# A decoder block on one core: two value blocks of the local attention by seven products, bias rows over all partitions, value read-outs behind the next split

## The chip, the cores and the metric

The kernel runs on one core of a Trainium2 chip. The metric is device microseconds of one execution. Engines are named as in the profile: PE is TensorE, DVE is VectorE, ACT is ScalarE, POOL is GpSimd, SP is the engine that issues most loads.

## The reference

One layer of a decoder block for 256 tokens (T) of width 2048 (D). All input projections are columns of one matrix `w_in` of 2048 x 19472:

```python
h = rms_norm(x, g_pre[l])
proj = h @ w_in[l]
y_a = pool_mixer(a_val, a_gate, w_pool[l], pool_scale[l])
y_b = swa_mixer(sq, sk, sv, s_gate)
y_c = gla_mixer(cq, ck, cv, c_lr, c_gate, w_alpha[l], b_alpha[l], g_gla[l])
y_m = mem_attn(mq, m_gate, mem, g_mem[l], w_mem_kv[l])
gates = sigmoid(g_logits.reshape(B, S, 4, 2048) + b_merge[l])
merged = sum of gates[:, :, b] * (y_b @ w_br_b[l]) over the four branches
x = x + rms_norm(merged @ w_out[l], g_post[l])
```

Two parts matter here. The values `sv` of the local (dilated window) attention are `h` times 1536 columns: three blocks of 512 columns, one for each window group. The logits of the gates, `g_logits`, are `h` times 8192 columns: 16 blocks of 512, four for each of the four branches, and `b_merge` is added to them.

## The kernel before, in words

**Numbers.** All large products are computed from float32 operands split into a high and a low part of a reduced type (`R`). A product is three matmuls: high by high, high by low, low by high (`mm3`, L156 to L160). A weight tile of 128 x 1024 is split by `split_w` (L149): ACT copies it to the high part (L152), DVE subtracts to get the low part (L153). There are five buffers for each part (`NB_HILO`, L30), so DVE can be at most five splits ahead of PE. Weights arrive by SP's queue as tiles `raw` of 1 MB (`load_raw`, L144); they share 13 buffers of 8 KB per partition (`e8`) with the normed input and other long-lived tiles.

**Main work.** It is written out as a row of units. `a_block` (L162) makes 256 tokens x up to 512 columns: for each of four weight tiles two splits, and for each split the two halves of the tokens, which accumulate in two PSUM tiles. For 512 columns it takes 16 x 2 x 3 = 96 matmuls of 512 columns and 8 splits. It returns `finish`, which reads both accumulators out. With the argument `late` it calls an earlier block's `finish` behind its own first split (L171 to L174). `b_unit` (L197) makes 128 columns with the weights standing: 16 matmuls of 512 and 16 of 256 columns, two splits, and a read-out of one or more DVE sums. The order is: the memory tokens; eight units cq and ck; the blocks cv0, cv1 and cv2 (values of the linear attention, L700 to L702, each read out at once by ACT, L550); units cg; mq and mg; av and ag (pooling); the blocks sv0, sv1 and sv2 (L835); and 28 units sq, sk and sg. Then come the merges (`bmem`, `bgla`, `bpool`, `bswa`) and the output.

**Two streams woven in.** While the main work runs, two others are advanced. `pull` (L91) steps a queue of small tasks: the chunks of the linear attention (`gla`), heads, pooling groups. `gates` (L109) advances the gate stream: a piece of main work of so many microseconds by plan earns `GATE_SHARE` (L34, 1.13) times as much credit, and each step of the stream costs credit (0.8 or 6.6). The stream starts after the sixth of the units cq and ck and is emptied ahead of the merges (`gates(1e9)`, L897).

**A gate pair** (`gate_pair`, L463) makes two blocks of 512 columns for both halves of the tokens, 2 x 2 products over 2048 = 2 x 1024 rows, by seven products of half size instead of eight (Strassen's scheme in Winograd's form). It has three parts. First p1 (L471 to L481): 16 steps of three matmuls, eight splits `gu`; after half of them ACT copies p1 aside (`p1c`, L480), and the later ones add on in the same PSUM tile. Then eight steps `gt` (L486 to L501): a 1 MB tile of weights, DVE sums on it (L491 with 1024 elements, L492 and L497 with 512 each), two splits, twelve matmuls into q4 to q7. Then sums of the products on DVE (L503 to L509), and two tiles `gv` (L510 to L518), four splits, added to q5. The results go through ACT's tanh (L459) and ACT's queue to memory in HBM, from where the merges read them back by POOL's queue (L918). A pair takes 168 matmuls of 512 columns, and 28 splits.

**The bias.** Ahead of the products, p1 and q5 are started with a matmul that adds the bias (`bias`, L453): its weights are one column of `sel`, repeated 128 times, its other operand is `brow`; both have 48 rows (16 with the high part of the bias, 16 empty, 16 with the low part). There are 16 such matmuls.

Of the kernel before, what the change touches and what calls it, by code (L numbers as in the profile page):

```python
# [8 lines left out]
F32 = mybir.dt.float32  # L9
R = mybir.dt.float32r  # L10
AF = mybir.ActivationFunctionType
ALU = mybir.AluOpType
# [20 lines left out]
NB_C2 = 7  # L33
GATE_SHARE = 1.13  # L34


@with_exitstack
def kernel(ctx, tc, ins, out):
# [388 lines left out]

    brow = cst.tile([48, 512], R, name="brow")
    sel = cst.tile([48, 24], R, name="sel")

# [3 lines left out]
    def bias_prep():  # L434
        pool.tensor_copy(walpha[:, 0:1], xcol[0:16, 0:1])
        pool.tensor_copy(big_cst[:, 0:1], xcol[:, 0:1])
        pool.dma_start(walpha[:], ins["w_alpha"])
        pool.dma_start(big_cst[:], ins["consts"])
        raw = c2("braw", [48, 512])
# [12 lines left out]

    def bias(o, r):  # L453
        ten.matmul(o, lhsT=sel[:, r : r + 1].to_broadcast([48, P]), rhs=brow[:], start=True, stop=False)

# [6 lines left out]

    def gate_pair(b, jj):  # L463


        j0, j1, n = 2 * jj, 2 * jj + 1, f"{b}{jj}"
        w = ins["w_g"]
        p1 = seven(f"p1{n}")
        bias(p1[:], 4 * b + j0)
        p1c = c2(f"p1c{n}", [P, 512])  # L470
        for u in range(4):  # L471
            raw = load_raw(w[b, j0, u], 2048)
            for hf in range(2):
                hi, lo = split_w(raw[:, hf * 1024 : (hf + 1) * 1024], 1024, f"gu{n}{u}{hf}")
                for i in range(2):
                    k = 4 * u + 2 * hf + i
                    ws = slice(i * 512, (i + 1) * 512)
                    mm3(p1[:], *tok(0, k), hi[:, ws], lo[:, ws], False, k % 8 == 7, k >= 8)
                if u == 1 and hf == 1:
                    act.activation(p1c[:], p1[:], AF.Copy)  # L480
                yield 0.8  # L481
        c11 = c2(f"c11{n}", [P, 512])
        put_gate(b, j0, 0, p1[:], c11[:])
        q4, q5, q6, q7 = [seven(f"q{i}{n}") for i in (4, 5, 6, 7)]
        bias(q5[:], 16 + 2 * b + jj)
        for kk in range(8):  # L486
            raw = new_raw()
            r4 = raw[:].rearrange("p (j u c) -> p j u c", j=2, u=2)
            u, cs = kk // 4, slice((kk % 4) * 512, (kk % 4 + 1) * 512)
            sync.dma_start(r4, w[b, j0 : j0 + 2, u : u + 3 : 2, :, cs].rearrange("j u p c -> p j u c"))  # L490
            vec.tensor_tensor(r4[:, :, 0, :], r4[:, :, 0, :], r4[:, 1, :, :], op=ALU.add)  # L491
# [6 lines left out]
            hi, lo = split_w(raw[:, 0:1024], 1024, f"gt{n}{kk}b")  # L498
            mm3(q5[:], *quart(0, kk), hi[:, 0:512], lo[:, 0:512], False, sp)
            mm3(q4[:], *tok(1, kk + 8), hi[:, 512:1024], lo[:, 512:1024], st, sp)  # L500
# [4 lines left out]
        vec.tensor_tensor(c21[:], q4[:], v3[:], op=ALU.subtract)  # L505
        put_gate(b, j0, 1, c21[:], c21[:])
        vec.tensor_tensor(v3[:], q5[:], v3[:], op=ALU.add)
        put_gate(b, j1, 1, v3[:], v3[:])
        vec.tensor_tensor(q5[:], q5[:], p1c[:], op=ALU.add)  # L509
        for u in range(2, 4):  # L510
            raw = load_raw(w[b, j1, u], 2048)
            for hf in range(2):
# [6 lines left out]
        c12 = c2(f"c12{n}", [P, 512])  # L519
        put_gate(b, j1, 0, q5[:], c12[:])  # L520
# [170 lines left out]
    for n in range(8):  # L691
# [404 lines left out]
```

## Time and profile before

| | |
|---|---|
| median of three runs | 1174.86 us (1171.3 to 1175.29) |
| profiled execution | 1172.68 us, of which the span of its instructions is 1170.6 |
| PE, DVE, ACT busy | 1149.8, 961.2, 647.0 us |
| from HBM | 303.94 MB by DMA, 260 GB/s in the mean |

The profile gives for each instruction its line, engine, and the tiles that it writes and reads (out<-in). A matmul's duration is its latency; how fast PE gets on is read from how far apart two matmuls start. The same holds for DVE, whose instructions overlap a little when they follow each other closely. The name of a split shows what it is for: `cv100h` is the high part of the first split of block cv1, `gt103bl` the low part of the second split of gate step 3 of branch 1, first pair (the digits after `gt` are branch, pair and step).

### The profile page before, as it was taken

The numbers are of one execution on the slowest core, as the hardware profiler recorded it, in microseconds if no ns is written. First come the engines' busy times: TensorE is split into PE (matmuls) and PEld (weight loads), VectorE is DVE, ScalarE is ACT, GpSimd is POOL, SyncE is SP. The second block draws the span as 40 slices with busy tenths as digits, with TensorE's granted clock in tenths as the row PEclk, the third lists the DMA queues.
The fourth block names the chain that finished last, engine by engine and source line by source line (L and its number), as shares of the span: only waits on it lengthen the run. The fifth ranks groups of instructions, "written<-read, shape, count | busy, mean of one in ns | idle before, by whom it ended". The sixth has DMA issues, their size and how long they took to land.

```text
span 1170.6 us, 15411 instructions
## 1 busy us (share of the span) xinstructions
PE 1149.8 (98%) x5854; PEld 968.2 (83%) x5854; DVE 961.2 (82%) x1201; ACT 647.0 (55%) x823; POOL 59.0 (5%) x109
## 2 busy tenths in 40 slices
PE   9999999999999999999999999999999999999997
PEld 7887898878888888878888887888788888888887
DVE  7979798999898799889989988987898676777454
ACT  7656456665655555665566556566555543434441
POOL 0010000000101001000000000000000102110000
PEclk9999999999999999999999999999999999999999
DMA  9755679757868688777788777876778988759321
GB/s 356 316 182 193 217 251 343 277 203 281 304 238 284 217 297 289 259 251 263 276 295 315 251 263 271 294 253 231 272 252 303 372 308 306 252 206 381 118 73 73
DMA packets 79946, 303.94 MB, mean 260 GB/s; under 512 B 6224, under 2 KB 8656, under 8 KB 57344
## 3 DMA queue, kind: packets, MB, share of 16 engines
q1 hardware_dynamic: 65568, 268.45, 63.5%
q0 software_dynamic: 8976, 24.91, 6.1%
q10 hardware_dynamic: 5328, 9.60, 2.2%
q8 instruction: 46, 0.75, 0.3%
q14 instruction: 28, 0.23, 0.1%
HBM read 285.11 MB, written 17.83 MB: 259 GB/s over the span
## 4 chain that ended last, share of the span: by engine, by line
PE 76%; DVE 5%; DMA 3%; ACT 2%; issue 2%; DVEq 0%; POOLq 0%; POOL 0%; ACTq 0%
PE q L158 5%; PE q L159 5%; PE q L160 5%; DMA raw<-in_w_g 2%; PE p L158 2%; PE p L159 1%; PE p L160 1%; PE sv2a L159 1%; PE sv0a L158 1%; PE sv0a L160 1%; PE o0a L160 1%; PE sv2a L158 1%; PE o0a L158 1%; PE sv1a L158 1%; PE sv0a L159 1%
## 5 line engine op out<-in xcount | busy, mean ns | idle before, releaser
L491 DVE TENSOR_TENSOR raw<-raw 128x1024 f32<-128x1024 f32 x64 | 78.1, 1220 | 8.9 <-DMA raw<-in_w_g 8.9
L497 DVE TENSOR_TENSOR raw<-raw 128x512 f32<-128x512 f32 x64 | 44.5, 696 | 1.1
L492 DVE TENSOR_TENSOR raw<-raw 128x512 f32<-128x512 f32 x64 | 44.5, 697 | 0.5
L918 POOL DMA_DIRECT2D g<-gd x32 | 17.4, 554 | 98.6 <-DVE merged L926 66.7
L926 DVE TENSOR_TENSOR merged<-merged,g 128x512 f32<-128x512 f32 x24 | 15.5, 686 | 0.0
L710 POOL DMA_DIRECT2D cgd<-cgate x4 | 2.2, 552 | 201.7 <-DVE cgate L241 201.7
L885 POOL DMA_DIRECT2D ybd<-ybt x4 | 2.7, 678 | 174.1 <-DVE ybt L247 174.1
L853 PE MATMUL sp<-k,q 128*128 128x128 f32 (+1 forms) x48 | 10.2, 335 | 1.0 <-DVE k L226 1.0
L861 ACT ACTIVATE s<-s,st 128x384 f32<-128x384 f32 (+1 forms) x8 | 6.2, 769 | 6.7 <-DVE st L860 6.7
L853 PEld LDWEIGHTS sp<-k,q 128*128 128x128 f32 x48 | 7.4, 190 | 2.9 <-DVE k L226 1.4
L856 DVE SCALAR_TENSOR_TENSOR s<-big_cst,sp 128x128 f32<-128x128 f32 (+1 forms) x24 | 7.1, 349 | 2.0 <-PE sp L853 2.0
L246 ACT ACTIVATE xhl<-xn 128x1024 fp32r<-128x1024 f32 x4 | 4.2, 1060 | 7.0 <-DVE xn L330 7.0
L459 ACT ACTIVATE c<-c 128x512 f32<-128x512 f32 x8 | 5.0, 628 | 5.5 <-DVE c L505 3.9
L939 ACT ACTIVATE mTh<-mtp 128x512 fp32r<-128x512 f32 x8 | 4.3, 595 | 6.3 <-PE mtp L937 6.3
L459 ACT ACTIVATE c<-p 128x512 f32<-128x512 f32 x8 | 4.7, 587 | 5.1 <-PE p L160 5.1
L664 POOL TENSOR_TENSOR ms<-ms,half 128x2 f32<-128x2 f32 x4 | 5.7, 1428 | 35.2 <-DVE ms L663 35.2
L879 PE MATMUL po<-pt,sv 128*128 128x256 f32 x24 | 7.2, 384 | 0.2 <-ACT pt L874 0.2
L812 POOL DMA_DIRECT2D yad<-yat x4 | 2.7, 686 | 88.5 <-DVE yat L247 88.5
L360 DVE SCALAR_TENSOR_TENSOR mhl<-mr,vecs,mhl 128x256 fp32r<-128x256 f32 x16 | 6.8, 479 | 0.4 <-issue 0.3
L652 POOL TENSOR_TENSOR sq<-sq 128x256 f32<-128x256 f32 x4 | 4.4, 1106 | 53.0 <-ACT sq L651 53.0
L359 ACT ACTIVATE mhl<-mr,vecs 128x256 fp32r<-128x256 f32 x16 | 6.9, 495 | 0.2 <-DMA mr<-in_memT 0.2
L1003 POOL TENSOR_TENSOR opart<-opart,half 128x1 f32<-128x1 f32 x2 | 1.1, 562 | 116.0 <-DVE opart L1002 116.0
(4603 smaller groups left out, 4582.7 us busy)
## 6 DMA issues: line engine op xcount, KB each, us to landing
raw<-in_w_g SPq DMA_DIRECT2D x112, 1024.0 KB, 5.8
raw<-in_w_sqk SPq DMA_DIRECT2D x24, 1024.0 KB, 6.6
raw<-in_w_sv SPq DMA_DIRECT2D x12, 1024.0 KB, 6.5
raw<-in_w_out SPq DMA_DIRECT2D x12, 1024.0 KB, 9.6
raw<-in_w_cqk SPq DMA_DIRECT2D x8, 1024.0 KB, 15.0
raw<-in_w_cg SPq DMA_DIRECT2D x8, 1024.0 KB, 6.6
raw<-in_w_av SPq DMA_DIRECT2D x8, 1024.0 KB, 5.0
raw<-in_w_ag SPq DMA_DIRECT2D x8, 1024.0 KB, 6.0
```

Source lines behind the costliest of these rows:

```text
L158: ten.matmul(o, lhsT=sh, rhs=wh, start=start, stop=False, skip_group_check=again)
L159: ten.matmul(o, lhsT=sh, rhs=wl, start=False, stop=False, skip_group_check=again)
L160: ten.matmul(o, lhsT=sl, rhs=wh, start=False, stop=stop, skip_group_check=again)
L459: act.activation(dst, src, AF.Tanh, scale=0.5)
L491: vec.tensor_tensor(r4[:, :, 0, :], r4[:, :, 0, :], r4[:, 1, :, :], op=ALU.add)
L492: vec.tensor_tensor(r4[:, 1, 1, :], r4[:, 1, 1, :], r4[:, 0, 0, :], op=ALU.add)
L497: vec.tensor_tensor(r4[:, 0, 1, :], r4[:, 0, 1, :], r4[:, 1, 1, :], op=ALU.add)
L853: ten.matmul(parts[g], lhsT=q3[:, g, it * P : (it + 1) * P], rhs=k3[:, g, :nj], start=True, stop=True)
L856: vec.scalar_tensor_tensor(s[:, g, :], dist[:, g, :], SLOPES[g * 4 + hh], parts[g], op0=ALU.mult, op1=ALU.add)
L879: ten.matmul(po[:], lhsT=sv[g][:, 0, vs], rhs=pt[g][:, 0:T], start=(g == 0), stop=False)
L918: pool.dma_start(gs[t][:], gate_dram[b, j, t][:])
L926: vec.tensor_tensor(m, m, gs[t][:], op=ALU.add)
```

## The change

1. The body of `gate_pair` becomes `seven_products(n, w, put, bias_rows)`, in which the store of a result (`put`) and the bias are parameters. `value_pair` calls it with the value blocks 0 and 1, without a bias, and stores the four results in HBM as they are. It is the fifth of nine pairs in the gate stream. The blocks sv0 and sv1 are no longer main work; sv2 stays. After sv2, the stream is advanced until the value pair is done (by the program's order it has been done by then), and POOL's queue reads the four results into the `sv` tiles.
2. `GATE_SHARE` is 1.38 instead of 1.13, and while sv2 runs `pull` takes twice as many steps.
3. `brow`, `sel` and the tiles that they are made from have 128 rows instead of 48; the additional ones are zero.
4. The blocks cv0 to cv2 are chained by `late`: a block is read out behind the first split of the next one.

```diff
-GATE_SHARE = 1.13
+GATE_SHARE = 1.38
...
+    rate = [1]
+
     def pull(n):
+        n *= rate[0]
...
-    brow = cst.tile([48, 512], R, name="brow")
-    sel = cst.tile([48, 24], R, name="sel")
+    brow = cst.tile([P, 512], R, name="brow")
+    sel = cst.tile([P, 24], R, name="sel")
...
-        one = c2("bsel", [48, 24])
-        vec.tensor_tensor(one[:, 0:16], ident[0:48, 0:16], ident[0:48, 32:48], op=ALU.add)
+        one = c2("bsel", [P, 24])
+        vec.tensor_tensor(one[:, 0:16], ident[:, 0:16], ident[:, 32:48], op=ALU.add)
...
-        ten.matmul(o, lhsT=sel[:, r : r + 1].to_broadcast([48, P]), rhs=brow[:], start=True, stop=False)
+        ten.matmul(o, lhsT=sel[:, r : r + 1].to_broadcast([P, P]), rhs=brow[:], start=True, stop=False)
...
+        def put(t, j, src, tmp):
+            put_gate(b, j0 + j, t, src, tmp)
+
+        return seven_products(f"{b}{jj}", ins["w_g"][b, j0 : j0 + 2], put, (4 * b + j0, 16 + 2 * b + jj))
+
+    sv_dram = {}
+
+    def value_pair():
+        def put(t, j, src, tmp):
+            if src is not tmp:
+                act.activation(tmp, src, AF.Copy)
+            sv_dram[j, t] = spill(f"svd{j}{t}", [P, 512], F32)
+            act.dma_start(sv_dram[j, t][:], tmp)
+
+        return seven_products("sv", ins["w_sv"][0:2], put, None)
+
+    def seven_products(n, w, put, bias_rows):
         p1 = seven(f"p1{n}")
-        bias(p1[:], 4 * b + j0)
+        if bias_rows:
+            bias(p1[:], bias_rows[0])
...
     def all_gates():
-        for jj in range(2):
-            for b in range(4):
-                yield from gate_pair(b, jj)
+        for n in range(9):
+            yield from value_pair() if n == 4 else gate_pair((n - (n > 4)) % 4, int(n > 4))
...
+    late = None
     for j in range(3):
         c0, n = CV_BLOCKS[j]
-        a_block(f"cv{j}", [ins[f"w_cv{j}"][u] for u in range(4)], h_at, n, cv_evac(j))()
+        late = a_block(f"cv{j}", [ins[f"w_cv{j}"][u] for u in range(4)], h_at, n, cv_evac(j), late=late)
+    late()
...
-    for j in range(3):
-        a_block(f"sv{j}", [ins["w_sv"][j, u] for u in range(4)], h_at, 512, sv_evac(j))()
+    rate[0] = 2
+    a_block("sv2", [ins["w_sv"][2, u] for u in range(4)], h_at, 512, sv_evac(2))()
+    while len(sv_dram) < 4:
+        gates(1.0)
+    for j, t in sv_dram:
+        pool.dma_start(sv[j][:, t, :], sv_dram[j, t][:])
...
+    rate[0] = 1
```

The order of the instructions is set when the program is built. At two places that the prediction speaks of, this is what stands there. First ACT, from the last splits of block cv0 to the first gate split after them, before:

```order
L152 ACTIVATE gt003bh<-raw_1291 128x1024
L152 ACTIVATE cv031h<-raw_1273 128x696
L550 ACTIVATE cv<-cv0a_1119 128x348
L550 ACTIVATE cv<-cv0a_1120 128x348
L152 ACTIVATE cv100h<-raw_1336 128x692
L152 ACTIVATE cv101h<-raw_1336 128x692
L152 ACTIVATE gt004ah<-raw_1370 128x1024
```

and now:

```order
L155 ACTIVATE gt004bh<-raw_1316 128x1024
L155 ACTIVATE cv031h<-raw_1298 128x696
L155 ACTIVATE cv100h<-raw_1359 128x692
L155 ACTIVATE cv101h<-raw_1359 128x692
L575 ACTIVATE cv<-cv0a_1144 128x348
L575 ACTIVATE cv<-cv0a_1145 128x348
L155 ACTIVATE gt005ah<-raw_1395 128x1024
```

Both splits of cv1's first tile moved ahead of the two read-outs of cv0 (L550, now L575), and the gate stream is one step further on. Second DVE, ahead of the first split of unit cg30 (`gq`, `kd` and `gk` belong to the linear attention, `cg21x` and `cgate` to the read-out of the unit before), before:

```order
L598 TENSOR_TENSOR gq<-gq,ep 128x1024
L491 TENSOR_TENSOR raw_2356<-raw_2356 128x2x512
L601 TENSOR_TENSOR kd<-bc 128x1024
L492 TENSOR_TENSOR raw_2356<-raw_2356 128x512
L491 TENSOR_TENSOR raw_2438<-raw_2438 128x2x512
L497 TENSOR_TENSOR raw_2356<-raw_2356 128x512
L153 TENSOR_TENSOR gt105al<-raw_2356,gt105ah 128x1024
L492 TENSOR_TENSOR raw_2438<-raw_2438 128x512
L226 TENSOR_TENSOR cg21x<-cg21a,cg21s 128x256
L153 TENSOR_TENSOR gt105bl<-raw_2356,gt105bh 128x1024
L241 SCALAR_TENSOR_TENSOR cgate_2222<-cg21t,cg21x 128x256
L153 TENSOR_TENSOR cg300l<-raw_2385,cg300h 128x1024
```

and now:

```order
L244 SCALAR_TENSOR_TENSOR cgate_2297<-cg20t,cg20x 128x256
L156 TENSOR_TENSOR gt107bl<-raw_2351,gt107bh 128x1024
L156 TENSOR_TENSOR cg210l<-raw_2377,cg210h 128x1024
L156 TENSOR_TENSOR cg211l<-raw_2377,cg211h 128x1024
L527 TENSOR_TENSOR p1c_1673<-q_1821,p1c_1673 128x512
L156 TENSOR_TENSOR gv1020l<-raw_2444,gv1020h 128x1024
L156 TENSOR_TENSOR gv1021l<-raw_2444,gv1021h 128x1024
L156 TENSOR_TENSOR gv1030l<-raw_2466,gv1030h 128x1024
L156 TENSOR_TENSOR gv1031l<-raw_2466,gv1031h 128x1024
L633 TENSOR_TENSOR gk<-gk,ep 128x1024
L229 TENSOR_TENSOR cg21x<-cg21a,cg21s 128x256
L156 TENSOR_TENSOR cg300l<-raw_2492,cg300h 128x1024
```

The second pair is two steps further on when cg30 begins: where its steps 5 and 6 stood, its last step and the four splits `gv` that end it now stand.

More of the change, by code (lines that the diff above doesn't have):

```diff
@@ L438, in bias_prep @@
         pool.dma_start(big_cst[:], ins["consts"])
-        raw = c2("braw", [48, 512])
+        raw = c2("braw", [P, 512])
         pool.memset(raw[:], 0.0)
@@ L463, in gate_pair @@
     def gate_pair(b, jj):
[L466 to L467 removed]
+        j0, j1 = 2 * jj, 2 * jj + 1
+        def put(t, j, src, tmp):
[10 more added lines that the diff above has]
+    def seven_products(n, w, put, bias_rows):
         p1 = seven(f"p1{n}")
[L469 removed]
+        if bias_rows:
+            bias(p1[:], bias_rows[0])
         p1c = c2(f"p1c{n}", [P, 512])
         for u in range(4):
[L472 removed]
+            raw = load_raw(w[0, u], 2048)
             for hf in range(2):
@@ L477, in gate_pair @@
                     ws = slice(i * 512, (i + 1) * 512)
-                    mm3(p1[:], *tok(0, k), hi[:, ws], lo[:, ws], False, k % 8 == 7, k >= 8)
+                    mm3(p1[:], *tok(0, k), hi[:, ws], lo[:, ws], k == 0 and not bias_rows, k % 8 == 7, k >= 8)
                 if u == 1 and hf == 1:
@@ L482, in gate_pair @@
         c11 = c2(f"c11{n}", [P, 512])
-        put_gate(b, j0, 0, p1[:], c11[:])
+        put(0, 0, p1[:], c11[:])
         q4, q5, q6, q7 = [seven(f"q{i}{n}") for i in (4, 5, 6, 7)]
-        bias(q5[:], 16 + 2 * b + jj)
+        if bias_rows:
+            bias(q5[:], bias_rows[1])
         for kk in range(8):
@@ L498, in gate_pair @@
             hi, lo = split_w(raw[:, 0:1024], 1024, f"gt{n}{kk}b")
-            mm3(q5[:], *quart(0, kk), hi[:, 0:512], lo[:, 0:512], False, sp)
+            mm3(q5[:], *quart(0, kk), hi[:, 0:512], lo[:, 0:512], st and not bias_rows, sp)
             mm3(q4[:], *tok(1, kk + 8), hi[:, 512:1024], lo[:, 512:1024], st, sp)
@@ L505, in gate_pair @@
         vec.tensor_tensor(c21[:], q4[:], v3[:], op=ALU.subtract)
-        put_gate(b, j0, 1, c21[:], c21[:])
+        done = c21[:]
+        put(1, 0, done, done)
         vec.tensor_tensor(v3[:], q5[:], v3[:], op=ALU.add)
-        put_gate(b, j1, 1, v3[:], v3[:])
+        done = v3[:]
+        put(1, 1, done, done)
         vec.tensor_tensor(q5[:], q5[:], p1c[:], op=ALU.add)
         for u in range(2, 4):
-            raw = load_raw(w[b, j1, u], 2048)
+            raw = load_raw(w[1, u], 2048)
             for hf in range(2):
@@ L519, in gate_pair @@
         c12 = c2(f"c12{n}", [P, 512])
-        put_gate(b, j1, 0, q5[:], c12[:])
+        put(0, 1, q5[:], c12[:])
     def all_gates():
-        for jj in range(2):
-            for b in range(4):
-                yield from gate_pair(b, jj)
+        for n in range(9):
+            yield from value_pair() if n == 4 else gate_pair((n - (n > 4)) % 4, int(n > 4))
     queue.append(("kmevac", km_evac()))
```

2 lines of the change are left out of this document (1 added, 1 removed).

## The prediction

> **What bounds the kernel now.** I read the page first, then busy times by window, then single stretches of the timeline. The page says who has no time left:
>
> ```profile
> span 1170.6 us, 15411 instructions
> PE 1149.8 (98%) x5854; PEld 968.2 (83%) x5854; DVE 961.2 (82%) x1201; ACT 647.0 (55%) x823; POOL 59.0 (5%) x109
> PEclk9999999999999999999999999999999999999999
> ```
>
> TensorE is busy for 98% of the span at full granted clock, so a matmul less is time less, as long as nobody keeps TensorE waiting. The next one is VectorE. Its share is an average over two different parts, so I take windows: the stretch in which the gate stream runs, two pieces of it, and the end of the stream.
>
> ```profile
> core 0: us, PE busy (x) PEld busy (x) DVE busy (x) ACT busy (x) POOL busy (x), PEclk, DMA share, GB/s
> 100.00:900.00 800.00, 791.26 (x4045) 666.00 (x4044) 708.43 (x873) 470.05 (x597) 28.92 (x47) 1.00 0.75 267
> 219.90:257.10 37.20, 36.00 (x184) 29.21 (x183) 36.12 (x46) 26.27 (x32) 1.13 (x2) 1.00 0.64 234
> 541.40:576.60 35.20, 35.20 (x159) 29.01 (x158) 32.91 (x46) 20.34 (x28) 2.36 (x7) 1.00 0.77 262
> 900.00:950.00 50.00, 49.48 (x260) 41.76 (x259) 33.14 (x44) 24.12 (x33) 5.88 (x11) 1.00 0.98 389
> ```
>
> From 100 to 900 us VectorE is busy for 88.6%. At 93.5% (541 to 577) TensorE lost nothing; at 97.1% (220 to 257, from cg10 to cg30, where the linear-attention steps fall on gate steps) it stood idle for 1.2 of 37.2 us. So the kernel is bound by TensorE, with VectorE close behind wherever gate steps are dense.
>
> **Products instead of blocks.** Two value blocks take 2 x 96 matmuls of 512 columns now. As a pair by seven products they take 48 + 96 + 24 = 168: 24 fewer. The price is how far apart they start:
>
> ```profile
> 607.29 0.39 PE L158 MATMUL q<-gv0131h,quarter 128*128 128x512 f32 x1
> 607.51 0.39 PE L159 MATMUL q<-gv0131l,quarter 128*128 128x512 f32 x1
> 607.74 0.39 PE L160 MATMUL q<-gv0131h,quarter 128*128 128x512 f32 x1
> 608.06 0.50 PE L454 MATMUL p<-brow,sel 48*128 48x512 f32 x1
> 608.49 0.50 PE L158 MATMUL p<-gu1100h,xhl 128*128 128x512 f32 x1
> 608.83 0.40 PE L159 MATMUL p<-gu1100l,xhl 128*128 128x512 f32 x1
> ```
>
> The first two starts lie 0.22 and 0.23 us apart (0.39 is the latency of one), so 24 x 0.227 = **5.4 us less**.
>
> **Bias rows.** The same rows show what a matmul of 48 rows costs. From 607.74 to 608.83 are three starts: 1.09 us, where three ordinary ones take 0.68. One bias matmul costs 0.41 us more than its columns: before it, after it, and at the matmul behind. Is it the rows, or that its weights are one column broadcast? The change keeps the broadcast. Another matmul with few rows, with no broadcast in it:
>
> ```profile
> 337.50 0.28 PE L209 MATMUL mg2a<-xhl,mg20l 128*128 128x256 f32 x1
> 337.61 0.39 PE L208 MATMUL mg2a<-xhl,mg20h 128*128 128x512 f32 x1
> 337.84 0.28 PE L209 MATMUL mg2a<-xhl,mg20l 128*128 128x256 f32 x1
> 338.05 0.48 PE L628 MATMUL pv<-cv,kt 64*128 64x256 f32 x1
> ...
> 339.11 0.50 PE L208 MATMUL mg2a<-xhl,mg21h 128*128 128x512 f32 x1
> 339.44 0.28 PE L209 MATMUL mg2a<-xhl,mg21l 128*128 128x256 f32 x1
> ```
>
> Into the 64 rows L209 takes 0.21 us instead of 0.11, and L208 behind them 0.33 instead of 0.23: the same two delays. So I put them down to the rows. There are 16 bias matmuls:
>
> ```profile
> L454 PE MATMUL p<-brow,sel x8: 492/497/498, 84.0 to 806.1; 48*128 48x512 f32 x8
> L454 PE MATMUL q<-brow,sel x8: 385/490/498, 84.4 to 808.3; 48*128 48x512 f32 x8
> ```
>
> Three pairs of p and q stand side by side (the first at 84.0 and 84.4) and share the way in and out: 13 x 0.41 = 5.3 us. Two of those overlap with waits for a split, so I take **4.9 us less**; the bounds are 0 (the broadcast is the reason) and 5.3. The Trainium skill, in "TensorE: Matmul & The Clock Gate", Step-by-step: what each phase is for, speaks against this edit: the time to load weights goes by the columns, "row count K doesn't matter here"; by it this term would be 0. The 80 more partitions of the tables cost nothing, since each instruction keeps its row length.
>
> **Read-outs behind the next split.** Before, ScalarE copies both halves of cv0 out ahead of splitting cv1's first weights:
>
> ```profile
> 139.66 0.46 ACT L550 ACTIVATE cv<-cv0a 128x348 f32<-128x348 f32 x1 [5.11 <-PE cv0a L160]
> 140.60 0.46 ACT L550 ACTIVATE cv<-cv0a 128x348 f32<-128x348 f32 x1 [0.48 <-PE cv0a L160]
> 140.96 0.77 ACT L152 ACTIVATE cv100h<-raw 128x692 fp32r<-128x692 f32 x1
> ...
> 145.38 1.06 ACT L152 ACTIVATE gt004ah<-raw 128x1024 fp32r<-128x1024 f32 x1 [2.97 <-issue]
> ```
> ```profile
> 140.09 0.32 PE L159 MATMUL cv0a<-cv031l,xhl 128*128 128x348 f32 x1
> 140.25 0.32 PE L160 MATMUL cv0a<-cv031h,xhl 128*128 128x348 f32 x1
> 141.78 0.59 PE L158 MATMUL cv1a<-cv100h,xhl 128*128 128x346 f32 x2 [1.22 <-ACT cv100h L152]
> 142.70 0.42 PE L159 MATMUL cv1a<-cv100l,xhl 128*128 128x346 f32 x1 [0.33 <-DVE cv100l L153]
> ```
>
> TensorE starts cv1 1.53 us after the last matmul of cv0 instead of 0.16, and the two matmuls up to 142.70 take 0.92 instead of 0.32: 2.0 us in all. With both splits ahead, what is late next is cv1's first accumulator, which must be read out first. That accumulator is finished six matmuls (0.95 us) before cv0 ends, and its copy takes 0.46 us, so it is out in time. Behind the waiting copies on ScalarE stands the split gt005ah, whose first matmul follows 24 of cv1 (3.8 us). I take **1.7 us less** (1.0 to 2.0). At cv1 to cv2 TensorE did not wait, so nothing is gained there.
>
> **What VectorE pays.** The pair adds 28 - 16 = 12 splits, 8 sums of 1024 elements, 16 of 512 and 5 at its end. Back to back they start so far apart:
>
> ```profile
> 213.96 1.22 DVE L153 TENSOR_TENSOR gt101al<-raw,gt101ah 128x1024 fp32r<-128x1024 f32 x1
> 215.10 1.22 DVE L491 TENSOR_TENSOR raw<-raw 128x1024 f32<-128x1024 f32 x1
> 216.23 1.22 DVE L153 TENSOR_TENSOR gt101bl<-raw,gt101bh 128x1024 fp32r<-128x1024 f32 x1
> ...
> 220.30 0.69 DVE L492 TENSOR_TENSOR raw<-raw 128x512 f32<-128x512 f32 x1
> ```
> ```profile
> 232.31 1.20 DVE raw L492 x2
> ```
>
> That is 1.13 us each for 1024 elements and 0.60 for 512: 20 x 1.13 + 21 x 0.60 = 35.2 us, all in the gate stretch. Its VectorE work becomes 743.6 us, in a stretch that the three gains shorten to 788: 94.4%, between the two windows above. Gate steps also stand closer together: in the stream's own units a step of 6.6 follows 6.6 / 1.38 = 4.8 of other work, and 6.6 / 1.13 = 5.8 before.
>
> Where does that bite? First where it bit already. By the order of the program, VectorE has 30 instructions of 1024 elements between its first split of cg10 and that of cg30, where it had 24: the pair's last splits now stand ahead of cg300l. TensorE has 113 matmuls of 512 columns there instead of 108. VectorE: 36.12 + 6 x 1.13 - 0.33 (one small sum less) = 42.6 us; TensorE: 36.0 + 5 x 0.227 = 37.1. The difference is 5.5 us, less what VectorE is ahead on entering; five pairs of split buffers allow some lead, but in the window of before a lead had not prevented 1.2 us of idling. I take **4.0 us more** (0 to 5.5). In the rest of the stretch, on a line between 93.5% with no loss and 97.1% with 3.2%, 94.4% would lose 0.8%, 5.6 us in 700; but a third of a pair's steps are plain products, in which TensorE is the longer side and VectorE catches up. I take **1.7 us more** (0 to 5.6).
>
> The ninth pair also has the wait for the copy of its half-finished product, on which p's next matmul stands:
>
> ```profile
> PE p L158 <- ACT p1c L480: 2.4, 4, 0.9
> ```
>
> Four of eight pairs waited, 2.4 us in all or 0.3 a pair; one more pair, and less other work between the steps, is **0.5 us more**.
>
> **Costed at nothing.** ScalarE gains 12 splits, at 1.06 us some 13 us on 470 of 800. The value products' four stores join ScalarE's queue, as the gates' do. Loads: six more of 1 MB.
>
> ```profile
> raw<-in_w_g SPq DMA_DIRECT2D x112, 1024.0 KB, 5.8
> ym<-ymd POOLq DMA_DIRECT2D x1, 1024.0 KB, 7.8
> g<-gd POOLq DMA_DIRECT2D x32, 256.0 KB, 4.7
> ```
>
> Eight MB more over 788 us are 11 GB/s on 267, below the 389 that the window from 900 shows. The four read-backs stand on GpSimd's queue behind the first pool spill and ahead of a memset and the weights of the next pool groups; they land in about 4.7 us, and their values are first read more than ten units later. If one of them were held up, the next pool group would be late by as much; its matmuls stand five units behind. At the stream's end one unit of 32 matmuls is left between the last gate matmul and the first merge, where two and a half were. The loads of the branch outputs hang on the last gate steps, some 110 matmuls (about 20 us) ahead of their use, and need 7.8; I take 0, or up to 2 us in a window whose DMA is already at 0.98.
>
> **The sum.** -5.4 - 4.9 - 1.7 + 4.0 + 1.7 + 0.5 = -5.8 us. The profiled execution took 1172.7 us (its span and 2.1 around it), so 1166.9 by it. The median of the runs shown is 2.2 above the profiled one: 1174.9 - 5.8 = **1169.1 us**. About 0.5%, 5.9 us, is what a measurement of this kernel can tell from no change; the forecast lies on that line.
>
> **Rivals.** *The lead covers all* (0.20): the split buffers carry VectorE through its dense stretches, as from 541 to 577. Then -5.4 - 5.3 - 2.0 + 0.5 = -12.2: 1162.7 us. For it: that window; against it: 1.2 us lost at 220 to 257 with less work.
>
> *VectorE becomes the bound* (0.15, slower): from 100 to 900 its 743.6 us have to fit. If waits for loads, copies and finished products let it be busy for only 92%, the stretch takes 808.3 us instead of 800, and the gains lie inside it: 1174.9 + 8.3 = 1183 us. It decides from 93.0% downwards (743.6 / 800). For it: 88.6% is all it reaches now. Against: that was all it was asked for, and both short windows exceed 93%.
>
> *The bias edit gives nothing* (0.17): the delay comes from the broadcast weights, not from the rows, and the starts behind a bias matmul stay as far apart. -5.8 + 4.9 = -0.9: 1174 us. Against it stand the rows of the 64-row matmul. The Trainium skill's sentence quoted above would make it so.
>
> **Chances.** Forecast 0.48, spread about its line; 0.26 of it counts as faster and 0.22 as the same. Faster: 0.26 + 0.20 = 0.46; same: 0.22 + 0.17 = 0.39; slower: 0.15. The range reaches from just below the full gain (1162.7) to the milder half of VectorE's bound: 1161 to 1180. The forecast's own bounds, with every cost at one end or the other, are 1162.7 and 1182.
>
> **What would show it.** Right: the starts around a bias matmul 0.23 us apart; no wait of TensorE for cv100h; TensorE idle for 4 to 7 us between cg10 and cg30 behind splits of VectorE, whose share there is 97% or more; VectorE's share of 100 to 900 at 93 to 95%. Wrong: a bias matmul that still costs 0.41 us; TensorE waiting in the value pair itself or at the first merge; or VectorE's share below 93% with TensorE idle more than before.

## The result and the profile after

| | before | after |
|---|---|---|
| median | 1174.38 us (4 runs, 1171.3 to 1175.29) | 1191.86 us (4 runs, 1191.24 to 1192.56) |
| ratio after to before | | 1.0154 (95%: 1.0134 to 1.0174) |
| profiled execution, span | 1172.68, 1170.6 | 1191.24, 1189.5 |
| TensorE's long pauses | 17.1 us | 34.4 us |
| half clock ahead of the tail | none | 23.8 us in four stretches |

The change made the kernel slower by 17.5 us, 11.9 beyond the upper end of the range. One execution among all runs below, the profiled one of e6, ran at a granted clock of 0.56 (1897.9 us) and stands in no number. The two last rows of the table are worked out from all matmuls of the trace. A pause is what the distance of two starts has beyond the usual one (0.227 us for 512 columns, 0.117 for 256, 0.158 for 346 or 348); those over 0.25 us are summed, and at half clock twice the usual distance is taken off. The tail is the last 3 to 6 us, at half clock in every profiled execution. The page of after:

```profile
span 1189.5 us, 15441 instructions
PE 1151.3 (97%) x5830; PEld 970.1 (82%) x5830; DVE 996.9 (84%) x1242; ACT 655.2 (55%) x834; POOL 61.9 (5%) x113
...
PEclk9999999999999999999899999899999999999999
```

The matmuls are 24 fewer, as announced, and VectorE has 35.7 us more (35.2 were forecast), but two slices of the row PEclk now show an 8. Three rows of busy times follow, with the columns of the table in the prediction: after from 100 to 900 us; before from the first split of cg10 to the first of cg30; after for the same piece of work:

```profile
100.00:900.00 800.00, 776.45 (x3938) 653.26 (x3937) 724.03 (x889) 466.37 (x594) 30.53 (x48) 0.99 0.76 270
```
```profile
217.37:257.86 40.49, 39.13 (x197) 31.48 (x196) 39.41 (x51) 27.83 (x34) 1.13 (x2) 1.00 0.61 221
```
```profile
221.85:269.75 47.90, 42.63 (x202) 32.68 (x201) 46.33 (x55) 31.30 (x37) 1.13 (x2) 0.96 0.64 236
```

VectorE's share from 100 to 900 us is 90.5% and not 94.4%: the stretch grew instead. From cg10 to cg30 it is 96.7% (97.3% before), and that piece takes 7.4 us longer with five matmuls (1.1 us) more. The waits of TensorE, in total, times and longest:

```profile
PE p L161 <- ACT p1c L503: 3.2, 2, 2.6
PE sk01a L212 <- DVE sk010l L156: 3.1, 1, 3.1
PE q L162 <- DVE gt311al L156: 2.3, 1, 2.3
PE cg20a L212 <- DVE cg200l L156: 2.2, 1, 2.2
PE sp L885 <- DVE s L888: 2.1, 1, 2.1
PE bmem0a L161 <- DVE sg3x L229: 1.8, 1, 1.8
PE p L161 <- ACT gu2100h L155: 1.6, 1, 1.6
```

In each of the seven rows stands a wait of 1.6 to 3.1 us, where before had none over 1.2. The prediction had looked at the places of cg20a, bmem0a (the first merge) and p1c; the other four fall into its 1.7 us for VectorE elsewhere. Behind all but cg20a stands a queue whose head waits. First three waits of VectorE, then two of what SP waits for between 545 and 567 us:

```profile
DVE raw L515 <- DMA raw<-in_w_g: 9.9, 7, 3.7
DVE s L888 <- DMA yad<-yat: 5.2, 1, 5.2
DVE win L799 <- DMA yad<-yat: 4.0, 1, 4.0
```
```profile
SPq L149 <- DVE gu0101l L156: 9.6, 1, 9.6
...
SPq L514 <- DVE ag001l L156: 1.9, 1, 1.9
```

One of these pauses can be followed from end to end (rows picked from the timeline of after, in order of time):

```profile
557.28 0.47 ACT L754 ACTIVATE ms<-mp,mst 128x256 f32<-128x256 f32 x1 [4.96 <-DMA ymd<-ymt]
558.34 0.17 DVE L757 RECIPROCAL mst<-mst 128x2 f32<-128x2 f32 x1 [3.06 <-ACT ms L754]
559.29 1.23 DVE L156 TENSOR_TENSOR gu0101l<-raw,gu0101h 128x1024 fp32r<-128x1024 f32 x1
560.54 0.33 SPq L149 DMA_DIRECT2D raw<-in_w_ag  x1
562.81 1.51 SPq L514 DMA_DIRECT2D raw<-in_w_g  x2
569.68 1.23 DVE L515 TENSOR_TENSOR raw<-raw 128x1024 f32<-128x1024 f32 x1 [2.35 <-DMA raw<-in_w_g]
570.82 0.42 DVE L229 TENSOR_TENSOR ag00x<-ag00a,ag00s 128x256 f32<-128x256 f32 x1
571.27 0.42 ACT L243 ACTIVATE ag00t<-ag00x 128x256 f32<-128x256 f32 x1 [2.16 <-DVE ag00x L229]
571.60 0.58 ACT L503 ACTIVATE p1c<-p 128x512 f32<-128x512 f32 x1
572.23 0.79 PE L161 MATMUL p<-gu0120h,xhl 128*128 128x512 f32 x1 [2.56 <-ACT p1c L503]
572.82 0.63 PE L162 MATMUL p<-gu0120l,xhl 128*128 128x512 f32 x1
573.25 0.63 PE L163 MATMUL p<-gu0120h,xhl 128*128 128x512 f32 x1
```

ScalarE wants a 2 KB buffer for a memory head (`ms`) which the store of another head still reads: 4.96 us. VectorE stands behind it for 3.06, and so splits gu0101 late. SP's next load needs the buffer that this split sets free, and is issued at 560.54 after 9.6 us of waiting. The load behind it (562.81) needs the buffer of ag001l, two splits further back in VectorE's queue; it lands at 569.6, and VectorE, at its first sum, waits for it for 2.35 us. Behind that sum stands the read-out ag00x, behind this on ScalarE a tanh, behind the tanh p1c, and on p1c TensorE: 2.56 us. Then its clock is halved, and starts lie 0.43 us apart instead of 0.23. It is a circle: VectorE's splits release the loads, so a wait of VectorE comes back some ten us later as a late load.

The two small edits did in the trace of after what was forecast of them:

```profile
144.42 0.32 PE L163 MATMUL cv0a<-cv031h,xhl 128*128 128x348 f32 x1
144.57 0.32 PE L161 MATMUL cv1a<-cv100h,xhl 128*128 128x346 f32 x1
...
650.00 0.40 PE L457 MATMUL p<-brow,sel 128*128 128x512 f32 x1
650.24 0.40 PE L457 MATMUL q<-brow,sel 128*128 128x512 f32 x1
650.47 0.39 PE L161 MATMUL q<-gv0120h,quarter 128*128 128x512 f32 x1
```

cv1 starts 0.15 us after the last matmul of cv0, and a bias matmul of 128 rows is one like any other.

### The profile page after: what moved, and what is told of

It is laid out like the page before. It is cut to its first block, busy times and chain, and to the rows that moved or that the text cites. A ratio compares the mean times of both kernels' runs of the same rounds, so it can differ in the third digit from the quotient of the medians.

```text
span 1189.5 us, 15441 instructions
## 1 busy us (share of the span) xinstructions
PE 1151.3 (97%) x5830; PEld 970.1 (82%) x5830; DVE 996.9 (84%) x1242; ACT 655.2 (55%) x834; POOL 61.9 (5%) x113
## 4 chain that ended last, share of the span: by engine, by line
PE 74%; DVE 9%; issue 8%; DMA 6%; ACT 3%; POOL 0%; SPq 0%; DVEq 0%; POOLq 0%; ACTq 0%
PE q L162 5%; PE q L161 5%; PE q L163 5%; DMA raw<-in_w_g 2%; DMA yad<-yat 2%; PE p L161 1%; PE p L163 1%; PE p L162 1%; PE kma L390 1%; DMA raw<-in_w_br_gla 1%; DVE raw L515 1%; DMA raw<-in_w_km 1%; PE sv2a L162 1%; PE sv2a L163 1%; PE sv2a L161 1%
## 5 line engine op out<-in xcount | busy, mean ns | idle before, releaser
L515 DVE TENSOR_TENSOR raw<-raw 128x1024 f32<-128x1024 f32 x72 | 89.2, 1241 | 10.8 <-DMA raw<-in_w_g 9.9
L521 DVE TENSOR_TENSOR raw<-raw 128x512 f32<-128x512 f32 x72 | 49.5, 687 | 1.1
L516 DVE TENSOR_TENSOR raw<-raw 128x512 f32<-128x512 f32 x72 | 49.2, 686 | 0.9
L950 POOL DMA_DIRECT2D g<-gd x32 | 17.3, 545 | 104.4 <-DVE merged L958 64.4
L754 ACT ACTIVATE ms<-mp,mst 128x256 f32<-128x256 f32 x8 | 3.7, 470 | 7.1 <-DMA ymd<-ymt 5.0
L799 DVE TENSOR_TENSOR win<-win 128x512 f32<-128x512 f32 x6 | 4.1, 686 | 4.0 <-DMA yad<-yat 4.0
L776 POOL DMA_DIRECT2D ymd<-ymt x4 | 2.7, 673 | 90.4 <-DVE ymt L250 90.4
```

Of the source, the lines that this page charges most:

```text
L516: vec.tensor_tensor(r4[:, 1, 1, :], r4[:, 1, 1, :], r4[:, 0, 0, :], op=ALU.add)
L521: vec.tensor_tensor(r4[:, 0, 1, :], r4[:, 0, 1, :], r4[:, 1, 1, :], op=ALU.add)
L950: pool.dma_start(gs[t][:], gate_dram[b, j, t][:])
```

## The experiments

The first theory was that the value pair does the harm, by waits that TensorE feels and the half clock behind them; the rivals were named as the runs left them open: the small edits, the work that VectorE gets, the closer steps, tasks that come late, the depth of the buffers. All runs stand in one table. The ratio is to the kernel before, timed beside each run; where runs were not timed together, differences below are differences of ratios times 1173 us. Pauses and half clock (tail left out) are from the profiled executions; e6 has the range of four runs and no profile.

| run | median us | ratio (95%) | pauses us | half clock us |
|---|---|---|---|---|
| e1_bias | 1171.31 | 0.9987 (0.9978 to 0.9996) | 19.6 | 0 |
| e2_late | 1168.64 | 0.9968 (0.9956 to 0.9981) | 13.4 | 0 |
| e3_both | 1166.71 | 0.9955 (0.9943 to 0.9968) | 16.8 | 0 |
| e4_pair | 1196.78 | 1.0205 (1.0182 to 1.0228) | 36.5 | 23.9 |
| e5_share | 1184.21 | 1.0104 (1.0089 to 1.0119) | 28.7 | 10.2 |
| e6_no_sums | 1189.24 to 1196.80 | 1.0166 (1.0135 to 1.0196) | | |
| e7_plain | 1189.53 | 1.0140 (1.0112 to 1.0168) | 30.7 | 6.8 |
| e8_rate3 | 1196.37 | 1.0200 (1.0174 to 1.0226) | 38.9 | 20.4 |
| e9_share127 | 1180.59 | 1.0074 (1.0057 to 1.0091) | 24.6 | 6.8 |
| e10_staged | 1198.32 | 1.0218 (1.0196 to 1.0240) | 42.8 | 17.0 |
| e11_staged2 | 1183.14 | 1.0097 (1.0078 to 1.0115) | 32.4 | 3.4 |
| e12_raw12 | 1256.50 | 1.0688 (1.0658 to 1.0717) | 78.8 | 51.0 |
| e13_hilo6 | 1259.82 | 1.0720 (1.0678 to 1.0761) | 84.8 | 57.8 |
| e14_c4 | 1249.04 | 1.0626 (1.0594 to 1.0658) | 74.7 | 37.4 |
| e15_share110 | 1175.27 | 1.0001 (0.9984 to 1.0018) | 23.3 | 10.2 |
| e16_raw14 | 1198.48 | 1.0216 (1.0188 to 1.0244) | 39.2 | 23.8 |
| e17_both14 | 1182.86 | 1.0081 (1.0055 to 1.0108) | 26.8 | 10.2 |
| e18_both12 | 1199.40 | 1.0220 (1.0195 to 1.0245) | 37.6 | 13.6 |

### Which part does the harm

e1 is before with the bias edit, e2 with the read-outs chained, e3 with both, e4 the change without these two:

```diff
# e1, e3
-    brow = cst.tile([48, 512], R, name="brow")
+    brow = cst.tile([P, 512], R, name="brow")
...
# e2, e3
-        a_block(f"cv{j}", [ins[f"w_cv{j}"][u] for u in range(4)], h_at, n, cv_evac(j))()
+        late = a_block(f"cv{j}", [ins[f"w_cv{j}"][u] for u in range(4)], h_at, n, cv_evac(j), late=late)
...
# e4, from the change
-    brow = cst.tile([P, 512], R, name="brow")
+    brow = cst.tile([48, 512], R, name="brow")
...
-        late = a_block(f"cv{j}", [ins[f"w_cv{j}"][u] for u in range(4)], h_at, n, cv_evac(j), late=late)
+        a_block(f"cv{j}", [ins[f"w_cv{j}"][u] for u in range(4)], h_at, n, cv_evac(j))()
```

> The kernel before with the bias rows on 128 partitions alone. Theory A (the value pair does the harm: it brings VectorE and ScalarE into waits that TensorE feels, and the clock halves behind those): this edit keeps its own gain, starts 0.23 us apart around each bias matmul, 4.9 us less, so about 1169.5 us against 1174.4, with no half clock ahead of the tail. Rival B (the gains of the small edits are spent again wherever they fall, since the engines behind TensorE set the pace): the starts are 0.23 us apart but the time stays within 2 us of before.

> The kernel before with the value read-outs of cv0 to cv2 behind the next block's first split, alone. Theory A: TensorE starts cv1 0.16 us after the last matmul of cv0 and the time falls by 1.7 us, to about 1172.7. Rival B: no change (1174.4), since VectorE and ScalarE are the later ones further on.

> The kernel before with the bias rows and the read-outs, without the value pair: share 1.13, sv0 to sv2 as blocks. Theory A: 6.6 us less, about 1167.8 us, and the fastest of all kernels so far; long pauses of TensorE stay near the 17 us of before. Rival B: within 2 us of 1174.4.

> The value pair alone (with its share of 1.38 and the doubled pull during sv2); bias rows on 48 partitions and read-outs of cv as before. Theory A: all the loss is here. The whole change came out 17.5 us slower with 6.6 us of gains in it, so about 1174.4 + 17.5 + 6.6 = 1198 us, with 30 us or more of long pauses and some 20 us at half clock. Rival B: the two small edits bring VectorE's work closer together and so are part of the harm: below 1190 us.

The harm is all in the value pair with its share: 24.0 us by the ratio of e4. The small edits are worth 1.5 and 3.8 us, and 5.3 together, and e3 has the lowest time of this study. By its time e1 falls to rival B (within 2 us), though its starts are as theory A had them; e2 and e3 do not.

The bias edit gives a third of the 4.9 us. Here is why, at the pair of bias matmuls near 394 us; before, then e1:

```profile
393.70 0.28 PE L209 MATMUL ag31a<-xhl,ag310l 128*128 128x256 f32 x1
393.91 0.50 PE L454 MATMUL p<-brow,sel 48*128 48x512 f32 x1
394.25 0.39 PE L454 MATMUL q<-brow,sel 48*128 48x512 f32 x1
395.01 0.50 PE L158 MATMUL p<-gu3000h,xhl 128*128 128x512 f32 x1 [0.37 <-ACT gu3000h L152]
```
```profile
395.21 0.28 PE L209 MATMUL ag31a<-xhl,ag310l 128*128 128x256 f32 x1
395.32 0.39 PE L454 MATMUL p<-brow,sel 128*128 128x512 f32 x1
395.56 0.40 PE L454 MATMUL q<-brow,sel 128*128 128x512 f32 x1
396.52 0.49 PE L158 MATMUL p<-gu3000h,xhl 128*128 128x512 f32 x1 [0.57 <-ACT gu3000h L152]
```

The two bias matmuls are through sooner, and the wait behind them is longer: 1.31 us from the first row to the last in both. Before and e1 have the same matmuls in the same order, so each can be set against itself: e1 gains 0.3 to 0.4 us at most bias matmuls, about 4 us in all, and gives back about as much: 1.2 at 212 us, where TensorE now waits for ScalarE to read out a gate, 1.1 from 332 to 336, and 0.8 each at 518 and 706; at 832, too, 1.2 are gained. In e2 the same comparison shows 2.1 us gained from cv0 to cv1 and 0.8 more at gt004, whose splits stand behind the read-outs on ScalarE. Then 0.8 are given back at 518 us, as in e1, and 0.9 gained at 832; 3.6 are left at the end.

### Load, spacing, or late tasks

e5 is e3 with the share of the change; e6, e7 and e8 start from the change.

```diff
# e5, from e3
-GATE_SHARE = 1.13
+GATE_SHARE = 1.38
# e6 (so for the three sums of a step)
-            vec.tensor_tensor(r4[:, :, 0, :], r4[:, :, 0, :], r4[:, 1, :, :], op=ALU.add)
+            if bias_rows:
+                vec.tensor_tensor(r4[:, :, 0, :], r4[:, :, 0, :], r4[:, 1, :, :], op=ALU.add)
# e7: value_pair as two plain blocks, 16 splits
-        return seven_products("sv", ins["w_sv"][0:2], put, None)
+                            mm3(accs[t][:], sh[:, ts], sl[:, ts], hi[:, ws], lo[:, ws], k == 0, k == KT - 1)
+                    yield 3.9
# e8
-    rate[0] = 2
+    rate[0] = 3
```

> The kernel with bias rows and read-outs but without the value pair (sv0 to sv2 as blocks), and with the share raised from 1.13 to 1.38: the eight gate pairs stand closer together and end sooner. Theory S (closer gate steps alone bring the pauses): about half of the pair's 24 us, so 1175 us or more against 1166.7 with the share of 1.13, with TensorE pauses over 2 us and a half clock behind them. Theory L (the work that the pair adds to VectorE) and theory Q (queued tasks that come later): 1167 to 1170 us.

> The whole change, with the three VectorE sums in each of the value pair's eight steps left out (8 of 1024 elements and 16 of 512, 18.6 us of VectorE; the values come out as others). Theory L (load): half of the pair's VectorE work of 35.2 us goes, and so does half or more of the 24 us: 1180 us or less. Theory S (spacing) and theory Q (late tasks): the pauses at 245 to 256, 550 to 580 and 740 to 755 us have nothing to do with these sums: 1188 us or more.

> The whole change, with the two value blocks in the same place of the gate stream and for the same credit, but as plain products: 192 matmuls instead of 168, 16 splits instead of 28, no sums. Theory L: VectorE has 35.2 us less, the loss is gone, and TensorE has 24 matmuls (5.4 us) more: about 1191.9 - 24 + 5.4 = 1173 us. Theory S and theory Q: the stream's spacing and the order of the tasks are the same, so the pauses stay: 1190 us or more.

> The whole change, with three times the pulls during sv2 instead of twice: 24 as in the three blocks of before, so that the pooling groups come 8 steps sooner and give their buffers back. Theory Q: the waits from 650 to 755 us (a head's scores waiting for a buffer that a pooling group's store still holds) go, and the half clock behind them: 8 to 13 us less, 1179 to 1184 us. Theory S and theory L: within 3 us of 1191.9.

The first of these matters most: e5 has not one instruction of the pair, only gate steps for which more credit is paid, and is 17.5 us slower than e3. Its timeline shows the pause of the change at 572 us again, on the same wait, 1 us later:

```profile
570.63 1.23 DVE L491 TENSOR_TENSOR raw<-raw 128x1024 f32<-128x1024 f32 x1 [2.07 <-DMA raw<-in_w_g]
571.77 0.42 DVE L226 TENSOR_TENSOR ag00x<-ag00a,ag00s 128x256 f32<-128x256 f32 x1
572.23 0.42 ACT L240 ACTIVATE ag00t<-ag00x 128x256 f32<-128x256 f32 x1 [1.77 <-DVE ag00x L226]
572.55 0.58 ACT L480 ACTIVATE p1c<-p 128x512 f32<-128x512 f32 x1
573.18 0.51 PE L158 MATMUL p<-gu1120h,xhl 128*128 128x512 f32 x1 [2.17 <-ACT p1c L480]
```

And the piece from cg10 to cg30, in e5 and in e3, next to the 47.90 and 40.49 of the change and of before:

```profile
221.15:269.32 48.17, 42.88 (x202) 32.91 (x201) 46.32 (x56) 31.30 (x37) 1.13 (x2) 0.96 0.64 236
```
```profile
215.28:255.53 40.25, 38.38 (x192) 30.46 (x191) 39.34 (x51) 27.33 (x33) 1.13 (x2) 1.00 0.64 223
```

So that loss belongs to the share. The work that the pair gives VectorE is at most the smaller part of the cause: without 18.6 us of its sums (e6) the ratio stays where it was, and with plain products in its place (e7) the kernel gains 1.6 us on the change, with 5.4 us more of matmuls; theory L had 1173 us. Those 1.6 and 5.4 us, some 7, may be the price of that work; the intervals of the two ratios leave some 4 us either way. Earlier tasks (e8) do not help either; the ratio is higher, 1.0200.

### By degrees, or by place

e9 and e15 are e3 at other shares, e10 and e11 the change with a share by stage:

```diff
# e9; e15 has 1.10
-GATE_SHARE = 1.13
+GATE_SHARE = 1.27
# e10; e11 has 1.45 and 1.31 for the last two
-        credit[0] += GATE_SHARE * work
+        credit[0] += share[0] * work
...
+    share[0] = 1.7
     late = None
...
     late()
+    share[0] = 1.0
...
+    share[0] = 1.38
     ym_dram = [spill("ymd", [P, 2, 4, T], R)]
...
+    share[0] = 1.38
     rate[0] = 2
```

> Bias rows and read-outs, no value pair, with the share at 1.27, between 1.13 (1166.7 us) and 1.38 (1184.2). Theory S1 (the loss comes in by degrees, as VectorE's lead over TensorE shrinks from a median of 3.9 us to 3.2): in between, 1174 to 1179 us. Theory S2 (each share puts other steps side by side, and a collision at one place makes the loss): anywhere from 1167 to 1184 us, with the pauses at other places than with 1.38.

> Bias rows and read-outs, no value pair, with the share at 1.10 instead of 1.13. If the loss grows by degrees with the share from 1.13 to 1.27 (14 us for 0.14), it should still fall below: 1163 to 1165.5 us, the fastest kernel. If at 1.13 VectorE's lead covers what there is: 1166 to 1168 us, no difference.

> The whole change, with a share by stage: 1.7 during cv0 to cv2, 1.0 during the cg units, 1.38 after that. Theory S1 (gate steps too dense where VectorE has other work): during cg VectorE has 35 us of other work on 45 us of units, during cv 22; the pauses from 200 to 270 us (7.7 us) and the half clock at 250 (1.7 us lost) go, and the later ones stay as they are: 1180 to 1185 us. Theory S2 (collisions): the later steps are shifted too, so the pauses after 300 us change place and size, and the time may come out anywhere from 1175 to 1195 us. If the pauses of cg only move to cv: 1190 us.

> As the run before with 1.7 and 1.0, but 1.45 from mq to ag and 1.31 from sv2 on. Theory S1: from 650 us on, where the whole change pauses for 13 us, the steps are less dense, and from 300 to 550, where it pauses for 1.4 us only, denser: 1174 to 1181 us, below the run before. Theory S2: no order between the two runs; the waits that a head's or a pooling group's buffer causes lie elsewhere again.

From 1.13 over 1.27 to 1.38 the ratio goes 0.9955, 1.0074, 1.0104, which looked like degrees, though not evenly spread. The share of 1.10 ended that: with steps further apart the ratio is 1.0001, 5.4 us above 1.13, with pauses elsewhere. Its profiled execution is the slowest of its ten (1180.52 us), so its trace may show more of them than another run has. The longest, by the waits of TensorE and of ScalarE:

```profile
PE sv0a L158 <- DVE ag01x L226: 3.2, 1, 3.2
```
```profile
ACT ag01s L224 <- DMA gd<-c: 3.6, 1, 3.6
```

A read-out wants a 2 KB buffer that a gate's store still holds, at 546 us. 1.13 and 1.38 have no such wait there; at 1.13 (e3) a gate's store holds up ScalarE for 1.7 us at 515 us. In e10 the pauses left the stretch from 200 to 270 only in part and came up during cv (3.8 us from 150 to 200, 0.4 in the change): 10.5 us from 100 to 300 against 9.9 in the change. e10 and e11 are the same up to mq, and 14 us apart. Theory S1 had 1180 to 1185 for e10 and missed by 13; theory S2, a collision at one place or another in each order, is what is left of the two; no run tests it by itself. Of the six orders tried with other shares (1.10, 1.27 and 1.38 without the pair; 1.38 and two staged ones with it), none came within 5 us of that at 1.13 by the ratios.

### How deep the buffers are

```diff
# e12, from the change; e18 the same, from e3
-NB_E8 = 13
+NB_E8 = 12
# e13 besides e12
-NB_HILO = 5
+NB_HILO = 6
# e14 besides e12
-NB_C4 = 9
+NB_C4 = 11
# e16, from the change; e17 the same, from e3
-NB_HILO = 5
-NB_E8 = 13
+NB_HILO = 4
+NB_E8 = 14
```

> The whole change with 12 instead of 13 buffers of 8 KB (weights as loaded, and long-lived tiles): the control for the next two. Theory B (the loss needs steps close together and shallow buffers: VectorE has too short a lead to cover a late load or a store that holds a buffer): loads come later, 3 to 8 us more, 1195 to 1200 us. Theory C (the order of the steps alone, whatever the buffers): within 3 us of 1191.9.

> As the run before, the 8 KB given to a sixth pair of split buffers. Theory B: VectorE's lead over TensorE grows by up to one split (about 2.7 us of TensorE), the pauses get shorter by that and some fall under the 2 us behind which the clock halves: 8 us or more below the run with 12 buffers, near 1187 us. Theory C: the same as that run.

> As the run with 12 buffers, the 8 KB given to two more buffers of 4 KB (scores, pooling, stores of branch outputs). Theory B: the waits of VectorE for a buffer that a pooling group's store still holds (4.0 and 5.2 us with the whole change) go, and so do pauses at 665 and 744 us with the half clock of 10 us behind the latter: 8 to 12 us below the run with 12 buffers. Theory C: the same as that run; or the next wait stands right behind.

> The whole change with 14 buffers of 8 KB instead of 13, and four pairs of split buffers instead of five, which gives the room. One large buffer less cost 64.6 us and a sixth split pair gained nothing. Theory D (the loads decide: SP can issue a load only when a split frees a large buffer, and VectorE meets loads that have not landed): loads come earlier, 8 us or more below 1191.9, 1184 us or less. Theory E (VectorE's lead decides, which four pairs make shorter by a split): 1200 us or more.

> Bias rows and read-outs, no value pair, share 1.13, with the same trade of a split pair for a fourteenth large buffer. Theory D: loads are early enough at this share already; 1163 to 1167 us against 1166.7. Theory E: 1172 us or more.

> Bias rows and read-outs, no value pair, share 1.13, with 12 large buffers. If the closer steps and the pair's six more loads are what makes the whole change need the depth, the loss is much smaller here than the 64.6 us there: 1166.7 + 10 to 30 us. If the depth is at its edge whatever the share: 1220 us or more.

One large buffer less costs the change 62.6 us by the ratios and e3 31.1. In both, 13 large buffers are just enough, and the change needs the last of them twice as much; that part of theory B held, its size (3 to 8 us) did not. A sixth split pair gained nothing (e13). Two more buffers of 4 KB brought 7.3 us, a little under the 8 to 12 expected; the wait of VectorE for the pooling store, 5.3 us in e12, is gone from the waits of e14:

```profile
DVE raw L515 <- DMA raw<-in_w_g: 32.7, 22, 4.1
...
DVE s L888 <- DMA yad<-yat: 5.3, 1, 5.3
```
```profile
DVE raw L515 <- DMA raw<-in_w_g: 35.1, 26, 4.1
...
DVE gu2000l L156 <- ACT gu2000h L155: 4.2, 1, 4.2
```

The trade of a split pair for a fourteenth large buffer lost in both kernels, 7.3 us in the change and 14.8 in e3; theory D fell, though the change paid half as much for it, and theory E came nearer (1198.5 us against 1200 or more, 1182.9 against 1172 or more). Part of this is not the gate stream's: by the traces e16 is 5.0 us behind the change, and e17 5.7 behind e3, at the first matmul of ck0, when the stream has not begun: TensorE waits 2.4 us for ScalarE (`mhl`) at 32 us and the clock is halved behind it. From there to the first merge e16 loses 5.3 us more and e17 11.2. So no exchange of buffers paid. That does not clear the loads or the lead in splits, since each exchange took from one what it gave the other, and the sixth split pair was tried with 12 large buffers only.

## Why the prediction was wrong

The forecast was 1169.1 us; 1191.9 came, which is also beyond the 1182 that the sum gave with every cost at its upper bound. By its own steps:

- **24 matmuls, 5.4 us less.** Right: 5830 for 5854, at the same distance.
- **Bias rows, 4.9 us less.** The cause was right: with 128 rows the delays are gone, broadcast or not, so the mechanism of the rival that the edit gives nothing is out. The size was wrong: 1.5 us arrived. Thirteen savings of 0.4 us were counted as path; in the trace of e1 about 4 us do arrive at the bias matmuls, and about as much goes again at later waits. The step allowed for two of the thirteen. The sentence quoted from the Trainium skill, "TensorE: Matmul & The Clock Gate", Step-by-step: what each phase is for, speaks of the time to load weights, and there the traces agree (0.18 us for 48 rows, 0.19 for 128; rows in the last section). What does not follow from it is that the term would be 0: the 0.41 us lie in the distance of the starts and not in the length of a load.
- **Read-outs, 1.7 us less.** Right in mechanism, too small: 3.8 (2.2 to 5.2). The upper bound of 2.0 stopped at cv1; the gate splits behind the copies on ScalarE's queue come sooner too.
- **cg10 to cg30, 4.0 us more (0 to 5.5).** Right in place and kind, with VectorE at 96.7% where 97% was named, and too small: TensorE lost 6.3 us more there (7.4 longer, 1.1 of it work), and up to 1.7 of those are the 3.4 us at half clock, which no step had. e5 confirms that it is the closer steps.
- **VectorE elsewhere, 1.7 us more (0 to 5.6).** This is the step that failed, and with it the price of the closer steps, which had no term of its own: e5 has 17.5 us for them. From 300 to 900 us the pauses grew from 6.8 to 18.0 us, and most of the half clock's 8.7 us come on top. The step took VectorE's share of busy time, found 94.4% between 93.5% without loss and 97.1% with 3.2%, and drew a line. The share turned out lower than at the window without loss, 90.5%, and the loss larger: what TensorE waited for was not VectorE at work but VectorE and ScalarE waiting in order behind a load or a held buffer.
- **The copy p1c, 0.5 us more.** The waits on it went from 2.4 to 3.2 us, but 2.6 of these are the pause followed above, which e5 shows without the ninth pair.
- **Costed at nothing.** Loads were judged by their mean rate (11 GB/s more on 267). It came to 270, which says nothing of when: a load can start only when a split frees its buffer. The stores of the pooling groups, which hold 4 KB buffers, were not costed at all. The first merge waited 1.8 us (bmem0a), inside the 2 us allowed.
- **The rival that VectorE becomes the bound** gave 1183 us by a share of 92%. Its sign and its words "waits for loads, copies and finished products" were nearer than the forecast, but its price came from the busy share too, and e6 and e7 show that taking VectorE's work away does not give the time back.
- **The signs.** Two that were named for wrong came: VectorE's share below 93% (90.5%) with TensorE idle for longer, and TensorE waiting in the value pair itself (1.2 us for gusv00l, 1.1 for q5sv).

The parts: e4 has 24.0 us for the pair where the sum had -5.4 + 4.0 + 1.7 + 0.5 = 0.8. With the 5.3 us of the small edits that makes 18.7; the change measured 18.1 by its ratio. Of the span's 18.9 us, 17.3 are longer pauses and 8.7 the half clock, against 5.4 of matmuls and 3.0 of short gaps saved: 17.6 together, with 1.3 not placed.

**What stays open.** The share by itself costs 17.5 us, against 24 for share and pair together, but not as a rate: 1.10 is worse than 1.13 as well. The pair at the share of 1.13 was not run, so what it costs without the closer steps is not known. Which orders are free of collisions was not settled by a rule, only that the one at 1.13 is nearly so, and that six others, with or without the pair, are not. How much of the rest is the pair's work and how much the new places of its stores and read-backs was not separated; e7 puts the work at about 7 us. The chain behind the pause at 572 us is read from the trace; more buffers of 2 KB, with which it begins, were not tried.

## What to carry to other kernels

Where two streams are woven by a planner and every engine works through its queue in order, a constant of the planner is not a neutral price for moving work: test it alone, without the work, before costing the work. A busy share says how much an engine has to do and not how long a wait it can cover; for that, follow the circle from a split to the buffer that it frees, to the load, and back to the next split. A gain on the path counts only up to the next wait behind it.

## What the runs showed of the hardware

TensorE's clock was halved at pauses well under 3.4 us: 2.37 us at 250 and 2.83 at 572 in the change, 2.03 in e15. The half-clock stretches last 3.4 us or multiples, and their starts in the change lie whole multiples of 3.41 us apart (250.1, 570.9, 745.0, 878.1: 94, 51 and 39 of them). Cut into such windows, the traces of e4, e5, e7, e9, e10, e11, e15 and the change show the pattern: where matmuls from 60 to 1000 us, counted at 0.2135 us for 512 columns (half of the 0.427 at half clock), left TensorE idle for 0.71 of a window at full clock or more, the next one was at half clock in 20 of 21 cases; from 0.65 to 0.67 in two of four; below in none. It need not be one pause: in e9 two of 1.6 us, ending at 274 and 276, left one window idle for 0.87, and the clock was halved behind it. So the 2 us in the expectation of e13 are no threshold: 2.33 us at 742 in e5 cost no clock. The pause of 3.29 us at 668 in the change lay across two windows (0.61 idle in the first) and cost no clock. The Trainium skill, "TensorE: Matmul & The Clock Gate", What's actually happening, has such a free-running window, but puts the drop behind an idle window of about 3.4 us; here 0.71 of one was enough in all cases but one.

A matmul of 48 rows among those of 128 cost 0.41 us beyond its columns (607.74 to 608.83 in before), one of 128 rows nothing (650.00 to 650.47 in after), with the same broadcast weights. Loading the weights took nearly the same time, before and then after (min, median and max in ns):

```profile
L454 PEld LDWEIGHTS p<-brow,sel x8: 182/182/183, 84.0 to 806.1; 48*128 48x128 f32 x8
```
```profile
L457 PEld LDWEIGHTS p<-brow,sel x8: 187/188/192, 84.7 to 843.8; 128*128 128x128 f32 x8
```

What differs is when a load starts: among matmuls of 128 rows 0.11 to 0.24 us ahead of its own matmul (649.89 for 650.00 in after, 608.59 for 608.83 in before), but for the 48 rows, and for the matmul behind them, together with it (608.06 and 608.49).
